# Second feed-forward: one 512-column product for the high and low parts of the token sums

## The chip, the core and the metric

The kernel runs on one core of one Trainium2 chip. The time is device microseconds for one launch of the whole block; the figure for a kernel is the median of several runs. The engines are TensorE (PE, matrix products), VectorE (DVE), ScalarE (ACT), GpSimd (POOL) and SyncE (SP, whose queue issues most of the DMA transfers here).

## What is computed

One layer of a streaming encoder block for 512 frames of width 1024: a feed-forward, a token mixer (a gated delta rule beside latent attention), and a second feed-forward, each behind a normalisation with a learned shift and scale, each added to the input with a gate:

```
x = x + 0.5 * g1 * swiglu(modulate(x, sh1, s1), ffn1_w_in, ffn1_w_out)
x = x + g2 * mixer(modulate(x, sh2, s2))
x = x + 0.5 * g3 * swiglu(modulate(x, sh3, s3), ffn2_w_in, ffn2_w_out)

swiglu(h, w_in, w_out): gate, up = split(h @ w_in); return (silu(gate) * up) @ w_out
```

`w_in` is 1024 x 5632 (2816 gate columns, 2816 up columns), `w_out` 2816 x 1024, all in float32. The change lies in the last line alone.

## The kernel before

Tokens lie along the columns of a tile (512 of them), features along the 128 partitions. Every float32 operand is split in two parts in the type fp32r: a high part by a cast, a low part by subtracting the cast from the original. A product of a 128 x 128 weight tile with an operand is three matmuls: high weight by high operand, high weight by low operand, low weight by high operand. They add up in PSUM, in tiles of 128 x 512 float32. There are eight such tiles: three in the pool that the method `acc` draws from (`pa` in the profile) and five in the pool of `aux` (`pb`).

**The pairs.** The 22 column blocks of gate and up are done one by one. The first four (`PLAIN`) are plain products. For each of the other 18, called pairs here and numbered 0 to 17 (f = 4 to 21 in the code), gate and up of both halves of the tokens are made from seven products of half the depth (four K tiles of 128) and half the width (256 tokens) in place of eight. For this the weight blocks `g` and `u` are loaded by SP into raw tiles (`wr`, 128 x 1024, a ring of four buffers), sums of their halves are made on DVE (`sx`, `sy`: `sums` and `sums2`), and `u`, the sums `x` and `y`, and half of `g` (`g1`) are split into high and low parts (`wh`/`wl`, `yh`/`yl`, `gh`/`gl`): in `pair_tasks`, `hi` is a cast on ACT and `lo` a subtraction on DVE. On the token side four sums `t1` to `t4` of four K tiles each are made once, in `token_sums`, with their high part in a tile `fh` and their low part in a tile `fl`; two sums share a pair of tiles, 256 columns each.

The seven products of a pair are named up0, up1, s2, s3, s1, s4 and gate1. Of these s2, s3, s1 and gate1 use token sums; up0, up1 and s4 use the plain token tiles (`hh`, `hl`). up0, s2, s1 and s4 add up in one half of a PSUM tile `A`; up1 takes one half of a second tile `BC`, and s3 and gate1 the other. On the way the state of `A` is copied out three times (`early_copy`), and `both`, `gate0`, `gate1`, `act1`, `act0` and `act_low` make from these the activation and its two parts (`ah`, `al`).

**The order.** `ffn2_rest` counts in ticks, and a pair begins every seven. `STEPS` says at which tick of a pair each product stands, so that one product of 12 matmuls of 256 columns stands in every tick; between them stand steps of the product with `w_out` (`k_step`: three matmuls of 512 columns into a `pa`). Pairs overlap: a pair's tasks stand from 11 ticks before its start (`load`) to 16 behind it (`act_low`). The list at the end of `pair_tasks` gives the tick of each. Tasks of one tick stand in the order in which they were added, and every engine works through its own instructions in the order of the program. SP's queue too is in order: a load that waits for its raw tile to come free holds all loads behind it. At the end of the pairs, the product with the last six blocks of `w_out` is woven in by the table `last` (`steps_of`), with accumulators from `acc`.

**A transfer that adds.** In earlier stages some low parts are made in another way, and the change uses it too (`split_w`): ACT writes the negated high part to the low tile with an activation (L195), and a DMA issued by POOL adds the raw tile to it (L196).

Lines that matter below, of the kernel before: L267 to L269 are the three matmuls of the product with `w_out`; L787 to L793 the sums of weights; L804 `hi`, L809 `lo`, L816 `early_copy`, L822 `both`, L825 `gate0`, L832 `act1`, L835 and L837 `act0`, L841 `act_low`, L872 to L874 the three matmuls of a product, L899 the addition of a finished column block to the result, L913 and L929 the split of `w_out`, L118 every load on SP.

## Time and profile before

| what | value |
|---|---|
| runs | 1047.45 us median of 3 (1047.32 to 1048.46) |
| profiled execution: its time | 1047.25 us |
| profiled execution: its span | 1045.6 us |
| mean granted TensorE clock | 0.999 |
| PE busy | 1029.0 us, 98% of the span |
| DVE, ACT, POOL busy | 682.6, 448.6, 48.2 us |

The span runs from the first to the last instruction that the profile holds, and the execution's own time has 1.65 us more around it. In a group of instructions, "x" is the count, then come busy time and mean duration, then the idle time of the engine just before. In a timeline the columns are start, duration, engine, line, operation, output and inputs. A duration is from start to end of one instruction; neighbours on one engine overlap a little, so the step from start to start is shorter than the duration. In the windows, "x" counts instructions, and DMA is the mean busy share of the 16 DMA engines. The pairs lie between 734 and 1010 us.

### The profile page before, as it was taken

The numbers are of one execution on the slowest core, as the hardware profiler recorded it, in microseconds if no ns is written. First come the engines' busy times: TensorE is split into PE (matmuls) and PEld (weight loads), VectorE is DVE, ScalarE is ACT, GpSimd is POOL, SyncE is SP. The second block draws the span as 40 slices with busy tenths as digits, with TensorE's granted clock in tenths as the row PEclk, the third lists the DMA queues.
The fourth block names the chain that finished last, engine by engine and source line by source line (L and its number), as shares of the span: only waits on it lengthen the run. The fifth ranks groups of instructions, "written<-read, shape, count | busy, mean of one in ns | idle before, by whom it ended". The sixth has DMA issues, their size and how long they took to land.

```text
span 1045.6 us, 16109 instructions
## 1 busy us (share of the span) xinstructions
PE 1029.0 (98%) x6379; PEld 882.2 (84%) x6379; DVE 682.6 (65%) x1251; ACT 448.6 (43%) x781; POOL 48.2 (5%) x113
## 2 busy tenths in 40 slices
PE   6999999999999999999999999999999999999998
PEld 4778878788887799888778779998999999999986
DVE  4488984333486636648878556788778778777633
ACT  4343222232222226749565464465345444344422
POOL 1000000000000011100010111310000000000000
PEclk9999999999999999999999999999999999999999
DMA  9989973323586439712212201173423334333222
GB/s 274 292 232 322 298 218 101 100 84 94 190 285 220 155 102 231 185 40 54 69 41 56 72 22 41 41 162 101 141 81 102 104 99 121 91 92 109 74 61 81
DMA packets 203689, 136.88 MB, mean 131 GB/s; under 512 B 13777, under 2 KB 186590, under 8 KB 203614
## 3 DMA queue, kind: packets, MB, share of 16 engines
q1 hardware_dynamic: 202318, 131.14, 42.6%
q0 software_dynamic: 1296, 4.72, 2.4%
q8 instruction: 50, 0.82, 0.3%
q14 instruction: 25, 0.20, 0.1%
HBM read 128.63 MB, written 2.49 MB: 125 GB/s over the span
## 4 chain that ended last, share of the span: by engine, by line
PE 90%; ACT 4%; DVE 4%; issue 1%; DMA 1%; POOL 0%; SPq 0%; POOLq 0%; ACTq 0%; DVEq 0%
PE pa L267 20%; PE pa L268 20%; PE pa L269 20%; PE pb L872 6%; PE pb L873 6%; PE pb L874 6%; PE pb L267 1%; PE pb L268 1%; PE pb L269 1%; PE pb L1909 1%; PE pb L418 1%; PE pb L1939 1%; PE pb L1494 1%; DVE cv L1438 1%; PE pb L1912 1%
## 5 line engine op out<-in xcount | busy, mean ns | idle before, releaser
L267 PE MATMUL pa<-hh,wh 128*128 128x512 f32 (+1 forms) x565 | 216.8, 384 | 0.4 <-ACT hh L465 0.4
L193 ACT CAST wh<-wr 128x1024 fp32r<-128x1024 f32 (+1 forms) x106 | 107.9, 1018 | 250.6 <-PE pa L268 177.8
L268 PE MATMUL pa<-hl,wh 128*128 128x512 f32 (+1 forms) x565 | 214.7, 380 | 0.5 <-DVE hl L457 0.3
L269 PE MATMUL pa<-hh,wl 128*128 128x512 f32 (+1 forms) x565 | 214.5, 380 | 0.0
L198 DVE TENSOR_TENSOR wl<-wr,wh 128x1024 fp32r<-128x1024 f32 (+1 forms) x97 | 114.2, 1178 | 104.0 <-ACT wh L193 101.6
L267 PE MATMUL pa<-ah,wh 128*128 128x512 f32 (+1 forms) x396 | 145.5, 368 | 0.6 <-DVE xT L899 0.4
L268 PE MATMUL pa<-al,wh 128*128 128x512 f32 (+1 forms) x396 | 144.5, 365 | 0.0
L269 PE MATMUL pa<-ah,wl 128*128 128x512 f32 (+1 forms) x396 | 143.5, 362 | 0.0
L267 PEld LDWEIGHTS pa<-hh,wh 128*128 128x128 f32 x565 | 106.4, 188 | 23.9 <-issue 3.3
L269 PEld LDWEIGHTS pa<-hh,wl 128*128 128x128 f32 x565 | 106.3, 188 | 20.6 <-issue 0.9
L268 PEld LDWEIGHTS pa<-hl,wh 128*128 128x128 f32 x565 | 106.5, 188 | 19.6 <-DVE hl L457 1.1
L269 PEld LDWEIGHTS pa<-ah,wl 128*128 128x128 f32 x396 | 74.8, 189 | 12.0
L267 PEld LDWEIGHTS pa<-ah,wh 128*128 128x128 f32 x396 | 75.2, 190 | 10.3 <-ACT wh L193 1.7
L268 PEld LDWEIGHTS pa<-al,wh 128*128 128x128 f32 x396 | 75.2, 190 | 7.2
L577 DVE SCALAR_TENSOR_TENSOR aa<-ar,sc,aa 128x512 f32<-128x512 f32 x98 | 72.9, 747 | 8.2 <-DMA ar<-in_w_ada 6.8
L872 PE MATMUL pb<-fh,wh 128*128 128x256 f32 x144 | 40.7, 283 | 0.0
L874 PE MATMUL pb<-fh,wl 128*128 128x256 f32 x144 | 40.7, 283 | 0.0
L874 PE MATMUL pb<-hh,wl 128*128 128x256 f32 x144 | 40.7, 283 | 0.0
L873 PE MATMUL pb<-fl,wh 128*128 128x256 f32 x144 | 40.7, 282 | 0.0
L873 PE MATMUL pb<-hl,wh 128*128 128x256 f32 x144 | 40.7, 282 | 0.0
L899 DVE SCALAR_TENSOR_TENSOR xT<-pa,mod,xT 128x512 f32<-128x512 f32 (+1 forms) x40 | 29.3, 735 | 17.3 <-PE pa L269 17.3
L872 PE MATMUL pb<-hh,wh 128*128 128x256 f32 x144 | 40.6, 282 | 0.0
(445 smaller groups left out, 2003.1 us busy)
## 6 DMA issues: line engine op xcount, KB each, us to landing
wr<-in_ffn_w_in SPq DMA_DIRECT2D x82, 512.0 KB, 3.9
ar<-in_w_ada SPq DMA_DIRECT2D x48, 512.0 KB, 6.1
wr<-in_ffn_w_out SPq DMA_DIRECT2D x34, 512.0 KB, 3.9
ar<-in_w_ada SPq DMA_DIRECT2D x48, 256.0 KB, 4.8
wr<-in_w_in SPq DMA_DIRECT2D x21, 512.0 KB, 4.3
wr<-in_ffn_w_out SPq DMA_DIRECT2D x17, 384.0 KB, 3.4
wl<-wr POOLq DMA_DIRECT2D x9, 512.0 KB, 6.1
wr<-in_w_out SPq DMA_DIRECT2D x8, 512.0 KB, 3.8
```

The lines of the kernel that those rows point to most:

```text
L193: self.nc.scalar.copy(hi, raw)
L198: self.nc.vector.tensor_tensor(out=lo, in0=raw, in1=hi.bitcast(F32), op=ALU.subtract)
L267: mm(out, wh, xh, start=start, stop=False)
L268: mm(out, wh, xl, start=False, stop=False)
L269: mm(out, wl, xh, start=False, stop=stop)
L418: nc.tensor.matmul(pg[32 * q:32 * q + 32, :256], self.sc[:, kc:kc + 1].to_broadcast([P, 32]), a[:, kc], start=(e == 0), stop=(e == 1), til ...
L577: nc.vector.scalar_tensor_tensor(out=acc, in0=a, scalar=sc, in1=acc, op0=ALU.mult, op1=ALU.add)
L872: mm(out, wh, xh, start=start and k == 0, stop=False, **kw)
L873: mm(out, wh, xl, start=False, stop=False, **kw)
L874: mm(out, wl, xh, start=False, stop=stop and k == 3, **kw)
L899: nc.vector.scalar_tensor_tensor(out=self.xT[t][:, ts], in0=p[:, ts], scalar=gate[:, t:t + 1], in1=self.xT[t][:, ts], op0=ALU.mult, op1=AL ...
L1438: nc.vector.scalar_tensor_tensor(out=a[:, d:], in0=p[:, :NT - d], scalar=wj(3 - d), in1=a[:, d:], op0=ALU.mult, op1=ALU.add)
```

## The change

- `token_sums` puts the high part of a token sum into the left half and the low part into the right half of one tile `fb`, one tile for each sum. The cast and the subtraction, one of 512 columns each before, are now two of 256 each.
- `product`: in s2, s3, s1 and gate1 the two matmuls with the high weight part become one of 512 columns, over the whole of `fb`. Its left half collects as before, and its right half collects what the low parts give. The matmul with the low weight part stays, with 256 columns. up0, up1 and s4 stay as they were.
- A PSUM tile now holds a product and its second half: `A` for up0, s2, s1 and s4; `U` (one half used) for up1, from `acc` in pairs with odd f and from `aux` in the others; `G` for s3 and gate1.
- The reads add the halves (`fold`, on DVE). Before, `both` was one operation of 512 columns; now it is three of 256. `gate0` becomes two instead of one, `act1` two instead of one, and the copy `uc` has a fold behind it. The third early copy (`cc`, right half) has a second copy on ACT and an addition on POOL behind it.
- The low part of `u` is no longer a subtraction on DVE: ACT negates `u` and writes it where the low part goes, and a DMA on POOL's queue adds the raw tile (`lo` does nothing for `u`). Here `hi` writes the activation with the scale -1 from the raw tile, in the type of the low part.
- The low part of `g1`, and `act_low` for all pairs but the last two, move from DVE to POOL.

```diff
--- before.py
+++ after.py
@@ -757,18 +757,19 @@
             stt(out=t[:, lo], in0=b[:, hi], scalar=self.dsh[:, k:k + 1], in1=a[:, hi], op0=ALU.add, op1=ALU.subtract)
             stt(out=t[:, hi], in0=b[:, lo], scalar=shift, in1=old[:, hi], op0=ALU.add, op1=ALU.subtract, reverse1=True)
             names = ("t3", "t4")
-        fh, fl = self.slot(F32R, "fh"), self.slot(F32R, "fl")
-        for name, part in zip(names, (lo, hi)):
-            self.T[name].append((fh[:, part], fl[:, part]))
-        nc.scalar.copy(fh, t)
-        yield
-        v.tensor_tensor(out=fl, in0=t, in1=fh.bitcast(F32), op=ALU.subtract)
+        both = [self.slot(F32R, "fb") for _ in range(2)]
+        for name, x, part in zip(names, both, (lo, hi)):
+            self.T[name].append((x[:, lo], x[:, hi], x))
+            nc.scalar.copy(x[:, lo], t[:, part])
+        yield
+        for x, part in zip(both, (lo, hi)):
+            v.tensor_tensor(out=x[:, hi], in0=t[:, part], in1=x[:, lo].bitcast(F32), op=ALU.subtract)
 
     def pair_tasks(self, f, base, add):
 
 
         nc, v, w = self.nc, self.nc.vector, self.ins["ffn2_w_in"][0]
-        r = {}
+        r = {"odd": f % 2}
         flat = lambda t: t.rearrange("p k f -> p (k f)")
         A, B = slice(0, NT), slice(NT, 2 * NT)
 
@@ -802,34 +803,52 @@
                     for e in "hl":
                         r[name + e] = flat(self.wp.tile([P, 8, P], F32R, tag="w" + e, name=self.name("w" + e)))
                 nc.scalar.copy(r[name + "h"], r[src][:, part])
+                if name in 'u':
+                    nc.scalar.activation(r[name + "l"], r[src][:, part], AF.Copy, scale=-1.0)
+                    nc.gpsimd.dma_start(r[name + "l"].bitcast(F32), r[src][:, part], accum_op=ALU.add)
             return go
 
         def lo(name, src, part=slice(0, 2 * NT)):
             def go():
-                v.tensor_tensor(out=r[name + "l"], in0=r[src][:, part], in1=r[name + "h"].bitcast(F32), op=ALU.subtract)
+                if name not in 'u':
+                    eng = nc.gpsimd if name == "g1" else v
+                    eng.tensor_tensor(out=r[name + "l"], in0=r[src][:, part], in1=r[name + "h"].bitcast(F32), op=ALU.subtract)
             return go
 
         def early_copy(name, part):
             def go():
                 if name not in r:
                     r[name] = self.slot(s=name)
-                nc.scalar.copy(r[name][:, part], r["A"][:, :HALF])
+                out = r[name][:, part]
+                nc.scalar.copy(out, r["A"][:, L])
+                if name == "uc":
+                    fold(out, out, r["A"][:, H])
+                elif part is H:
+                    nc.scalar.copy(r["uc"][:, H], r["A"][:, H])
+                    nc.gpsimd.tensor_tensor(out=out, in0=out, in1=r["uc"][:, H], op=ALU.add)
             return go
 
+        def fold(out, a, b):
+            v.tensor_tensor(out=out, in0=a, in1=b, op=ALU.add)
+
         L, H = slice(0, HALF), slice(HALF, NT)
 
         def both():
-            v.tensor_tensor(out=r["cc"], in0=r["cc"], in1=r["BC"], op=ALU.add)
+            for x in (L, H):
+                fold(r["cc"][:, H], r["cc"][:, H], r["G"][:, x])
+            fold(r["cc"][:, L], r["cc"][:, L], r["U"][:, L])
 
         def gate0():
-            v.tensor_tensor(out=r["uc"][:, H], in0=r["uc"][:, L], in1=r["BC"][:, H], op=ALU.add)
+            fold(r["uc"][:, H], r["uc"][:, L], r["G"][:, L])
+            fold(r["uc"][:, H], r["uc"][:, H], r["G"][:, H])
             nc.scalar.activation(r["uc"][:, H], r["uc"][:, H], AF.Silu, scale=-1.0)
 
         def gate1():
             nc.scalar.activation(r["cc"][:, H], r["cc"][:, H], AF.Silu, scale=-1.0)
 
         def act1():
-            v.tensor_tensor(out=r["cc"][:, H], in0=r["cc"][:, H], in1=r["A"][:, :HALF], op=ALU.mult)
+            fold(r["uc"][:, H], r["uc"][:, H], r["A"][:, L])
+            v.tensor_tensor(out=r["cc"][:, H], in0=r["cc"][:, H], in1=r["uc"][:, H], op=ALU.mult)
 
         def act0():
             v.tensor_tensor(out=r["cc"][:, L], in0=r["cc"][:, L], in1=r["uc"][:, H], op=ALU.mult)
@@ -838,7 +857,8 @@
 
         def act_low():
             al = self.slot(F32R, "al")
-            v.tensor_tensor(out=al, in0=r["cc"], in1=r["ah"].bitcast(F32), op=ALU.subtract)
+            eng = nc.gpsimd if f < FT - 2 else v
+            eng.tensor_tensor(out=al, in0=r["cc"], in1=r["ah"].bitcast(F32), op=ALU.subtract)
             self.act.append((r["ah"], al))
 
         r["do"] = dict(load=load, sums=sums, sums2=sums2)
@@ -857,20 +877,28 @@
 
 
         if "A" not in r:
-            r["A"], r["BC"] = self.aux(), self.aux()
+            r["A"] = self.aux()
+        if what == "up1":
+            r["U"] = self.acc() if r["odd"] else self.aux()
+        if what == "s3":
+            r["G"] = self.aux()
         L, H = slice(0, HALF), slice(HALF, NT)
-        b = lambda k0, ts: [(self.h[k][0][:, ts], self.h[k][1][:, ts]) for k in range(k0, k0 + 4)]
+        b = lambda k0, ts: [(self.h[k][0][:, ts], self.h[k][1][:, ts], None) for k in range(k0, k0 + 4)]
         out, w, part, xs, start, stop = {
-            "up0": (r["A"][:, L], "u", 0, b(0, L), True, False), "up1": (r["BC"][:, L], "u", 1, b(4, L), True, True),
-            "s2": (r["A"][:, L], "x", 1, self.T["t2"], False, False), "s3": (r["BC"][:, H], "x", 0, self.T["t3"], True, False),
-            "s1": (r["A"][:, L], "y", 0, self.T["t1"], False, False), "s4": (r["A"][:, L], "y", 1, b(4, H), False, True),
-            "gate1": (r["BC"][:, H], "g1", 0, self.T["t4"], False, True)}[what]
+            "up0": ("A", "u", 0, b(0, L), True, False), "up1": ("U", "u", 1, b(4, L), True, True),
+            "s2": ("A", "x", 1, self.T["t2"], False, False), "s3": ("G", "x", 0, self.T["t3"], True, False),
+            "s1": ("A", "y", 0, self.T["t1"], False, False), "s4": ("A", "y", 1, b(4, H), False, True),
+            "gate1": ("G", "g1", 0, self.T["t4"], False, True)}[what]
         mm, kw = self.nc.tensor.matmul, dict(skip_group_check=True)
-        for k, (xh, xl) in enumerate(xs):
+        wide, out = r[out], r[out][:, L]
+        for k, (xh, xl, both) in enumerate(xs):
             c = slice(part * NT + k * P, part * NT + k * P + P)
             wh, wl = r[w + "h"][:, c], r[w + "l"][:, c]
-            mm(out, wh, xh, start=start and k == 0, stop=False, **kw)
-            mm(out, wh, xl, start=False, stop=False, **kw)
+            if both is None:
+                mm(out, wh, xh, start=start and k == 0, stop=False, **kw)
+                mm(out, wh, xl, start=False, stop=False, **kw)
+            else:
+                mm(wide, wh, both, start=start and k == 0, stop=False, **kw)
             mm(out, wl, xh, start=False, stop=stop and k == 3, **kw)
 
     def ffn2_rest(self, ps):
```

**The products.** First two K tiles of s2 on PE, before (`fh`, `fl` the token sum's parts, `wh`, `wl` the weight's, `pb1416` the tile A):

```order
L872 MATMUL pb1416_7137<-fh1342_6867,wh1395_7070 128x256 [waits Activation_49]
L873 MATMUL pb1416_7137<-fl1343_6868,wh1395_7070 128x256
L874 MATMUL pb1416_7137<-fh1342_6867,wl1396_7071 128x256
L872 MATMUL pb1416_7137<-fh1345_6873,wh1395_7070 128x256
L873 MATMUL pb1416_7137<-fl1346_6874,wh1395_7070 128x256
L874 MATMUL pb1416_7137<-fh1345_6873,wl1396_7071 128x256
```

Now the same two K tiles and the two behind them (`fb` is a sum's tile with both parts):

```order
L901 MATMUL pb1416_7154<-fb1343_6868,wh1395_7085 128x512 [waits Activation_49]
L902 MATMUL pb1416_7154<-fb1343_6868,wl1396_7086 128x256
L901 MATMUL pb1416_7154<-fb1346_6875,wh1395_7085 128x512
L902 MATMUL pb1416_7154<-fb1346_6875,wl1396_7086 128x256
L901 MATMUL pb1416_7154<-fb1349_6884,wh1395_7085 128x512
L902 MATMUL pb1416_7154<-fb1349_6884,wl1396_7086 128x256
```

Three matmuls of 256 columns have become one of 512 and one of 256, with as many columns in all.

**The raw tile of u, pairs 5 and 6.** On DVE before: `wr1490` is the raw u of pair 5, read last by the subtraction L809.

```order
L791 SCALAR_TENSOR_TENSOR sx1496_7728<-sy1497_7729,wr1490_7656 128x512
L793 TENSOR_TENSOR sy1497_7729<-wr1490_7656,sx1496_7728 128x512 [waits DVE_49]
L809 TENSOR_TENSOR wl1503_7753<-wr1490_7656,wh1502_7752 128x1024 [waits Activation_49]
L832 TENSOR_TENSOR cc1482_7608<-cc1482_7608,pb1479_7584 128x256 [waits PE_49,Activation_49]
L809 TENSOR_TENSOR wl1509_7790<-sx1496_7728,wh1508_7789 128x1024 [waits Activation_49]
```

Now on POOL, where the same tile is `wr1493` and its last reader is the DMA that adds it to `wl1506`:

```order
L828 TENSOR_TENSOR cc1484_7605<-cc1484_7605,uc1494_7673 128x256 [waits Activation_49,Pool_49]
L815 TENSOR_TENSOR gl1499_7703<-wr1471_7502,gh1498_7702 128x512 [waits DMAHW2_49,PE_49,Pool_49]
L808 DMA wl1506_7743<-wr1493_7655 128x1024 [waits DMASW3_49,DMAHW5_49,PE_49,Activation_49]
L861 TENSOR_TENSOR al1508_7760<-cc1463_7452,ah1503_7735 128x512 [waits DVE_49]
L828 TENSOR_TENSOR cc1504_7740<-cc1504_7740,uc1516_7798 128x256 [waits Activation_49]
```

SP's loads at that place before; `wr1511` is the raw u of pair 6, and takes the buffer of `wr1490`:

```order
L118 DMA wr1490_7656<-in_ffn2_w_in 128x8x128 [waits DMAHW7_49,DVE_49]
L118 DMA wr1505_7772<-in_ffn2_w_out 128x4x256 [waits DMAHW3_49,DVE_49]
L118 DMA wr1510_7792<-in_ffn2_w_in 128x8x128 [waits DMAHW2_49,DVE_49]
L118 DMA wr1511_7794<-in_ffn2_w_in 128x8x128 [waits DMAHW5_49,DVE_49]
L118 DMA wr1526_7905<-in_ffn2_w_out 128x4x256 [waits DMAHW4_49,DVE_49]
```

And now; `wr1515` is the raw u of pair 6:

```order
L118 DMA wr1493_7655<-in_ffn2_w_in 128x8x128 [waits DMAHW7_49,Activation_49,Pool_49]
L118 DMA wr1509_7765<-in_ffn2_w_out 128x4x256 [waits DMASW5_49,DMAHW3_49,DVE_49,Activation_49]
L118 DMA wr1514_7784<-in_ffn2_w_in 128x8x128 [waits DMAHW2_49,Activation_49,Pool_49]
L118 DMA wr1515_7786<-in_ffn2_w_in 128x8x128 [waits DMASW6_49,DMAHW5_49,DVE_49,Activation_49]
L118 DMA wr1531_7891<-in_ffn2_w_out 128x4x256 [waits DMAHW6_49,DVE_49]
```

The subtraction has left DVE. The load of pair 6's u, which waited for a DVE instruction, now waits for a transfer on POOL's queue to land (`DMASW6`).

**Behind s1 of the last pair.** On PE before, from the last matmul of s1 to the first of `steps_of(2, 0, 2)`:

```order
L874 MATMUL pb1793_9792<-fh1358_6924,yl1786_9728 128x256
L267 MATMUL pa1805_9902<-ah1775_9655,wh1799_9830 128x512
L268 MATMUL pa1805_9902<-al1779_9678,wh1799_9830 128x512
L269 MATMUL pa1805_9902<-ah1775_9655,wl1800_9831 128x512
L267 MATMUL pa1805_9902<-ah1795_9807,wh1799_9830 128x512
L268 MATMUL pa1805_9902<-al1798_9827,wh1799_9830 128x512
L269 MATMUL pa1805_9902<-ah1795_9807,wl1800_9831 128x512
L267 MATMUL pa1809_9938<-ah1731_9329,wh1803_9868 128x512 [waits Activation_49]
```

And now; `pa1814` is U of the last pair (f = 21, odd), and `pa1827` the accumulator that takes its buffer:

```order
L902 MATMUL pb1810_9690<-fb1358_6930,yl1802_9634 128x256
L267 MATMUL pa1823_9793<-ah1790_9559,wh1816_9730 128x512
L268 MATMUL pa1823_9793<-al1795_9587,wh1816_9730 128x512
L269 MATMUL pa1823_9793<-ah1790_9559,wl1817_9731 128x512
L267 MATMUL pa1823_9793<-ah1811_9704,wh1816_9730 128x512
L268 MATMUL pa1823_9793<-al1815_9727,wh1816_9730 128x512
L269 MATMUL pa1823_9793<-ah1811_9704,wl1817_9731 128x512
L267 MATMUL pa1827_9830<-ah1744_9247,wh1820_9766 128x512 [waits DVE_49,Activation_49]
```

On DVE the folds of `both` for that pair stand so now, and the last of them is what the matmul waits for:

```order
L854 TENSOR_TENSOR cc1791_9564<-cc1791_9564,uc1800_9629 128x256
L832 TENSOR_TENSOR cc1812_9709<-cc1812_9709,pb1822_9769 128x256 [waits Pool_49]
L832 TENSOR_TENSOR cc1812_9709<-cc1812_9709,pb1822_9769 128x256 [waits DVE_49]
L832 TENSOR_TENSOR cc1812_9709<-cc1812_9709,pa1814_9714 128x256
L861 TENSOR_TENSOR al1828_9837<-cc1791_9564,ah1826_9825 128x512 [waits Activation_49]
```

The matmul that waited for ACT alone now waits for DVE too; DVE's first fold waits for the addition on POOL.

## The prediction

> **What bounds the kernel now.** I read the busy table first, then the chain of waits by engine, then windows over the pairs, with the slices of the DMA engines kept for later.
>
> ```profile
> PE 1029.0 (98%) x6379; PEld 882.2 (84%) x6379; DVE 682.6 (65%) x1251; ACT 448.6 (43%) x781; POOL 48.2 (5%) x113
> ...
> DMA  9989973323586439712212201173423334333222
> ...
> PE 90%; ACT 4%; DVE 4%; issue 1%; DMA 1%; POOL 0%; SPq 0%; POOLq 0%; ACTq 0%; DVEq 0%
> ```
>
> TensorE is busy for 98% of the span and carries 90% of the chain that ended last. The windows (PE, PEld, DVE, ACT and POOL busy, granted clock, DMA share, GB/s) say the same of the pairs:
>
> ```profile
> 800.00:820.00 20.00, 19.96 (x150) 18.98 (x149) 17.39 (x24) 9.78 (x17) 0.00 (x0) 1.00 0.43 132
> ...
> 840.00:900.00 60.00, 60.00 (x418) 55.99 (x417) 44.91 (x64) 26.09 (x44) 0.00 (x0) 1.00 0.35 105
> ```
>
> PE has no gap between 840 and 900 us, and 0.04 us between 800 and 820. So a gain can come only from less PE time, and what is taken off DVE gains nothing by itself. The other engines matter where they come so late that PE waits. The question is whether the change saves PE more than it makes it wait.
>
> **What PE saves.** The timeline of PE at the end of a step of the product with w_out, through s2, into the next step, and at six of these 512-column matmuls in the tail:
>
> ```profile
> 901.37 0.39 PE L269 MATMUL pa<-ah,wl 128*128 128x512 f32 x1
> 901.60 0.28 PE L872 MATMUL pb<-fh,wh 128*128 128x256 f32 x1
> ...
> 903.03 0.40 PE L267 MATMUL pa<-ah,wh 128*128 128x512 f32 x1
> ...
> 1004.87 0.28 PE L874 MATMUL pb<-fh,yl 128*128 128x256 f32 x1
> 1004.99 0.40 PE L267 MATMUL pa<-ah,wh 128*128 128x512 f32 x1
> ...
> 1006.37 0.39 PE L267 MATMUL pa<-ah,wh 128*128 128x512 f32 x1
> ```
>
> The 0.28 and 0.40 us are lengths; the pace is the step from start to start. Twelve matmuls of 256 columns take 903.03 - 901.60 = 1.43 us, 119 ns each. Six of 512 take 1006.37 - 1004.99 = 1.38 us, 230 ns each, and one with a 256 behind it 0.23 us (901.37 to 901.60). Two of 256 are 238 ns, so the merge saves 8 ns. There are 4 products x 4 K tiles x 18 pairs = 288 such places: 288 x 8 ns = 2.4 us. The starts are given to 10 ns; with a step of 235 ns the saving is 0.9 us, with 226 ns 3.5 us. I take 2.4.
>
> [...]
>
> **What the reads cost.** Durations before, by group (count, busy, mean ns, idle before), of DVE, then ACT, then POOL (in its earlier stages, since POOL does nothing in the pairs):
>
> ```profile
> L822 DVE TENSOR_TENSOR cc<-cc,pb 128x512 f32<-128x512 f32 x15 | 10.2, 679 | 0.0
> L809 DVE TENSOR_TENSOR gl<-wr,gh 128x512 fp32r<-128x512 f32 x15 | 10.4, 691 | 6.0 <-ACT gh L804 6.0
> L841 DVE TENSOR_TENSOR al<-cc,ah 128x512 fp32r<-128x512 f32 x15 | 10.4, 691 | 1.1
> L825 DVE TENSOR_TENSOR uc<-uc,pb 128x256 f32<-128x256 f32 x14 | 5.9, 420 | 23.5 <-PE pb L874 23.5
> ...
> L816 ACT COPY cc<-pb 128x256 f32<-128x256 f32 x30 | 11.0, 366 | 1.7 <-PE pb L874 1.5
> L195 ACT ACTIVATE wl<-wr 128x1024 fp32r<-128x1024 f32 x9 | 9.4, 1044 | 0.0
> ...
> L481 POOL TENSOR_TENSOR na<-na,sq 128x256 f32<-128x256 f32 x9 | 7.8, 868 | 112.0 <-ACT sq L479 111.9
> ```
>
> The starts of the sums of weights below give the pair's period, and show what slack s2 has in an ordinary pair:
>
> ```profile
> 832.90 0.68 DVE L788 TENSOR_TENSOR sx<-wr,wr 128x512 f32<-128x512 f32 x1
> 848.48 0.68 DVE L788 TENSOR_TENSOR sx<-wr,wr 128x512 f32<-128x512 f32 x1
> ...
> 835.61 0.37 ACT L816 COPY cc<-pb 128x256 f32<-128x256 f32 x1
> 836.58 1.06 ACT L804 CAST wh<-wr 128x1024 fp32r<-128x1024 f32 x1 [0.60 <-ACT cc L816]
> ...
> 839.28 0.28 PE L872 MATMUL pb<-fh,wh 128*128 128x256 f32 x1
> ```
>
> The period is 848.48 - 832.90 = 15.58 us. DVE works 44.91 / 60 x 15.58 = 11.7 us of it. The low parts of g1 and of the activation leave it (0.69 each), the low part of u too (1.22, the row of L809 below), and `both` goes from 0.68 to 3 x 0.42. The other folds add 3 x 0.42. Net: 10.9 us. ACT, at 26.09 / 60 x 15.58 = 6.8 us, gains a negation (1.04) and a copy (0.37). POOL gains 2 x 128x512, an addition (0.87) and a DMA issue. All fit in the period, and I cost them at nothing where PE's work covers them: s2 may start when the copy `cc` is done (835.61 + 0.37 = 835.98) but starts at 839.28, so it has 3.3 us of cover. Once that is used up, a delay costs PE its whole length. The two halves in `token_sums` lie ahead of the pairs, under plain products, and I leave them at nothing too.
>
> **The detour of u's low part.** The subtraction becomes a negation and a DMA. Times of the nine such DMAs in earlier stages (issue, and from issue to landing), then those of the loads between 795 and 860 us:
>
> ```profile
> L196 POOL DMA_DIRECT2D wl<-wr x9: 836/848/1038, 395.8 to 690.8; - x9
> ...
> DMA to landing us min/median/max: 4.5/6.1/8.7
> ```
>
> ```profile
> DMA to landing us min/median/max: 3.7/3.8/3.9
> ```
>
> For the product up0 of its own pair this comes early enough. In an ordinary pair the cast of u ends at 837.64 (836.58 + 1.06); with the negation and 6.1 us it lands at 844.8, ahead of up0 at about 848.5. But the raw tile stays held until the landing, and the next pair's u loads into it. That load then lands at 844.8 + 3.8 = 848.6, just when `sx` wants it (848.48). With 8.7 us `sx` would be 2.7 us late, which the 3.3 us of cover still take.
>
> One pair has no cover, since the table of ticks makes pair 4 to 5 short. Rows of SP, DVE, ACT and PE there:
>
> ```profile
> 794.31 5.75 SPq L118 DMA_DIRECT2D wr<-in_ffn_w_in  x2
> ...
> 798.44 1.22 DVE L809 TENSOR_TENSOR wl<-wr,wh 128x1024 fp32r<-128x1024 f32 x1
> 804.88 0.68 DVE L788 TENSOR_TENSOR sx<-wr,wr 128x512 f32<-128x512 f32 x1
> ...
> 796.64 1.05 ACT L804 CAST wh<-wr 128x1024 fp32r<-128x1024 f32 x1
> 807.59 0.36 ACT L816 COPY cc<-pb 128x256 f32<-128x256 f32 x1
> ...
> 808.01 0.39 PE L872 MATMUL pb<-fh,wh 128*128 128x256 f32 x1
> ```
>
> Before, L809 ended at 799.66 and let pair 6's u load go (the second of SP's two, ending at 800.06). Now the cast ends at 797.69, the negation at about 798.7, and the raw tile is free when the DMA has landed: at 803.2 with 4.5 us, at 807.4 with 8.7 us. I take 5.0. The nine were measured in slices where the DMA engines were mostly 7 to 9 tenths busy (slices 16, 17 and 27 of the row DMA above; one slice is 26.1 us), and here the share is 0.43, so I stay near the fast end. Then the load is in at 803.7 + 3.8 = 807.5, and `sx`, at 804.88 before, is 2.6 us late. Queued behind it on DVE are the low part of w_out and `act0`; ACT's `ah` waits for `act0`, the copy `cc` stands behind `ah` on ACT, and s2 waits for the copy: 807.59 + 0.36 = 807.95, and s2 began at 808.01. So the cover is 0.06 us, and PE waits **2.5 us** (2.0 to 6.2).
>
> **The tile U at the end.** In the tail `steps_of(2, 0, 2)` takes the buffer of the last pair's U, and waits until the third fold of `both` has read it. Rows of ACT and DVE, to stand beside PE's rows at 1004.87 to 1006.37:
>
> ```profile
> 1005.19 0.37 ACT L816 COPY cc<-pb 128x256 f32<-128x256 f32 x1 [1.22 <-PE pb L874]
> ...
> 1005.59 0.69 DVE L822 TENSOR_TENSOR cc<-cc,pb 128x512 f32<-128x512 f32 x1 [0.30 <-ACT cc L816]
> ```
>
> s1 ends, the copy stands at 1005.19, the second copy behind it from about 1005.46 to 1005.83, the addition on POOL to 1006.7 (0.87), and three folds of 0.42 with steps of about 0.33 to 1007.8. PE wanted the buffer at 1006.37: it waits about **1.5 us**. With a POOL addition half as long it is 1.1; with one twice as long, 2.4.
>
> **The sum.** -2.4 + 2.5 + 1.5 = +1.6 us, made against the profiled execution of 1047.25: 1048.85. The median of the runs is 0.2 above that execution, so I say 1049.0.
>
> **Rivals.**
>
> *Only the saving* (chance 0.20). The two waits do not come, since loads or buffers fall otherwise than I follow them. For the first that needs a landing before 801.1 us (807.95 would then hold), 2.4 us after the issue, and the shortest of nine was 4.5. For the second it needs another buffer for U. Price: 1047.45 - 2.4 = 1045.0, down to 1043.9 with the upper end of the saving.
>
> *One wait alone, or both with a larger saving* (0.15). The tail's wait alone gives 1047.45 - 2.4 + 1.5 = 1046.5; both with 3.5 us saved, 1048.0.
>
> *The transfer takes as long as the slowest of the nine* (0.12), so that pair 5 waits 6.2 us: 1047.45 - 2.4 + 6.2 + 1.5 = 1052.8. For it speaks that the negated tile is read and written by the transfer while loads run; against it, the share of 0.43. Here too belongs that 512 columns cost PE two times 256 and nothing is saved: 1051.4.
>
> *DVE and POOL block each other* (0.08). POOL now works in the pairs for the first time. The trace has a place where the two overlap, and one where they don't:
>
> ```profile
> 640.12 1.23 DVE L198 TENSOR_TENSOR wl<-wr,wh 128x1024 fp32r<-128x1024 f32 x1
> ...
> 640.28 1.96 POOL L1232 TENSOR_TENSOR Sg<-S,gl 128x512 f32<-128x512 f32 x1
> 646.96 1.04 POOL L1232 TENSOR_TENSOR Sg<-S,gl 128x512 f32<-128x512 f32 x1 [4.72 <-DVE S L1731]
> ```
>
> A 128x512 on POOL took 1.96 in place of 1.04 us beside a DVE subtraction with two inputs in SBUF. If every operation of POOL were stretched so (1.96 + 1.96 + 1.6) and DVE stood still for as long, DVE would need 10.9 + 5.5 = 16.4 us of a period of 15.58; it decides from 4.7 us a pair on. Then 0.8 us x 12 ordinary pairs = 9.8 us come on top: 1058.8. Against it: in that place it was POOL that stretched, and DVE's 1.23 was its usual 1.22. [...]
>
> **Chances.** Forecast 0.45, rivals 0.20, 0.15, 0.12 and 0.08. What a measurement can tell from no change is about 0.2%, or 2.1 us: 1045.35 to 1049.55. Below lies most of the first rival: 0.17. Within lie the second rival, the rest of the first and some 0.28 of the forecast (its own range, by the bounds of its terms without the longest landing, is 1047.5 to 1050.5): 0.46. Above lie 0.17 of the forecast and the last two rivals: 0.37. The range for eight in ten reaches from the first rival, 1044.8, to the third, 1053.0.
>
> **What would show it.** In the profile after: steps of 230 ns for L901 (PE busy lower by some 2 us over the pairs); one wait of PE at s2 of pair 5, near 808 us, with `sx` as the late link and SP's load behind the landing on POOL's queue; one wait of PE near 1006 us for a fold on DVE; no other wait of PE between 734 and 1000 us; DVE near 11 us a pair. Waits in every pair would make the last rival right. No wait at 808 us would mean that the raw tile is not the link that I take it for, and a landing above 6 us that the load on the DMA engines does not explain the spread.

## The result, and the profile after

The changed kernel takes 1051.51 us (median of 18 runs, 1050.03 to 1058.25), the kernel before 1047.53 in the runs beside it: a ratio of 1.0043, with a 95% interval of 1.0035 to 1.0052. It is slower by some 4 us, where 1.6 were forecast. The profiled execution of the changed kernel has a span of 1049.2 us against 1045.6, so there are 3.6 us to find between the two traces. The other 0.4 us of the 4.0 lie outside the spans: the changed kernel's execution has 1051.27 - 1049.2 = 2.07 us around its span, for 1.65 before, and the traces do not show what they are. One execution further below, of the kernel with a raw tile of its own, ran at a granted clock of 0.852 from end to end; it is the one that was profiled, and the ratio leaves it out.

The busy table and the chain of waits by engine, after:

```profile
PE 1028.8 (98%) x6091; PEld 868.6 (83%) x6091; DVE 706.6 (67%) x1297; ACT 468.6 (45%) x825; POOL 126.7 (12%) x183
...
PE 92%; DVE 2%; issue 2%; ACT 2%; DMA 1%; POOL 1%; SPq 0%; POOLq 0%; ACTq 0%; DVEq 0%
```

PE has the 288 matmuls less (6379 - 6091), and its busy time has not moved, though the chain still lies on it. So part of what it saved has come back as slower matmuls, and the span grew by waits on top. The waits of PE behind 734 us (what waited, for whom, total, times, longest):

```profile
PE pb L901 <- ACT cc L823: 3.2, 1, 3.2
PE pa L267 <- ACT cc L847: 1.5, 1, 1.5
PE pa L267 <- DVE xT L927: 0.5, 1, 0.5
PE pb L730 <- DVE xT L927: 0.4, 1, 0.4
```

The last two stood in the kernel before with 0.4 us each. New are one wait of 3.2 us and one of 1.5 us. The first is s2 of pair 5; rows of DVE, ACT, PE and POOL around it:

```profile
802.88 0.68 DVE L788 TENSOR_TENSOR sy<-wr 128x512 f32<-128x512 f32 x1
806.56 1.45 DVE L789 TENSOR_TENSOR sx<-wr,wr 128x512 f32<-128x512 f32 x1 [3.00 <-DMA wr<-in_ffn_w_in]
...
810.03 0.37 ACT L823 COPY cc<-pb 128x256 f32<-128x256 f32 x1
...
810.45 0.50 PE L901 MATMUL pb<-fb,wh 128*128 128x512 f32 x1 [3.24 <-ACT cc L823]
...
797.09 0.86 POOL L808 DMA_DIRECT2D wl<-wr  x1 [1.03 <-ACT wl L807]
806.17 1.29 POOL L815 TENSOR_TENSOR gl<-wr,gh 128x512 fp32r<-128x512 f32 x1
```

The sum `sx` of pair 6 waits for its raw tile's load (3.00 us of idle DVE), and the queue behind it brings s2 late by 3.24 us. Before, s2 began 808.01 - 804.88 = 3.13 us behind `sx`; now it is 810.45 - 806.56 = 3.89 us. The 0.76 us more are `sx` itself, which took 1.45 us for 0.68, beside the low part of g1 on POOL (806.17 to 807.46). So the late load makes some 2.5 us of the pause, and the stretched sum some 0.8.

The second is the matmul behind s1 of the last pair that takes the buffer of U; rows of POOL, DVE and PE:

```profile
1007.81 0.73 POOL L828 TENSOR_TENSOR cc<-cc,uc 128x256 f32<-128x256 f32 x1 [10.56 <-ACT uc L827]
1009.36 0.41 DVE L832 TENSOR_TENSOR cc<-cc,pa 128x256 f32<-128x256 f32 x1
1009.92 0.47 PE L267 MATMUL pa<-ah,wh 128*128 128x512 f32 x1 [1.49 <-ACT cc L847]
```

The third fold, which reads U, ends at 1009.77. The view names an ACT instruction (L847) because that one ended last; a run below shows that the matmul does not need it.

Behind the first pause comes what was not foreseen. Windows of one microsecond over the restart; the number behind POOL's busy time is the granted clock:

```profile
810.00:811.00 1.00, 0.55 (x3) 0.51 (x4) 1.00 (x3) 1.00 (x3) 0.00 (x0) 0.97 0.55 110
811.00:812.00 1.00, 1.00 (x5) 0.81 (x4) 0.97 (x3) 1.00 (x2) 0.00 (x0) 0.50 1.08 382
812.00:813.00 1.00, 1.00 (x5) 0.90 (x4) 0.61 (x2) 1.00 (x3) 0.40 (x1) 0.50 1.14 341
813.00:814.00 1.00, 1.00 (x3) 0.77 (x3) 0.22 (x2) 1.00 (x3) 1.00 (x2) 0.50 0.91 216
814.00:815.00 1.00, 1.00 (x5) 0.81 (x4) 1.00 (x2) 0.76 (x1) 0.79 (x1) 0.82 1.02 197
```

The clock is at half from about 810.94 (0.97 as a mean over a microsecond) to 814.36 (0.82): 3.42 us. What it costs is read from the steps of PE inside and behind it:

```profile
812.14 0.63 PE L901 MATMUL pb<-fb,wh 128*128 128x512 f32 x1
812.78 0.63 PE L267 MATMUL pa<-ah,wh 128*128 128x512 f32 x1
...
815.23 0.40 PE L901 MATMUL pb<-fb,wh 128*128 128x512 f32 x1
815.58 0.40 PE L901 MATMUL pb<-fb,wh 128*128 128x512 f32 x1
```

A wide matmul with the narrow one behind it takes 0.64 us at half clock and 0.35 at full, so 3.42 us do the work of 1.87, a loss of about 1.6 us. The other pairs run as planned. For the pace I compare the first matmul of up0 in pair 1 and in pair 17, before and after:

```profile
746.66 0.28 PE L872 MATMUL pb<-hh,wh 128*128 128x256 f32 x1
990.78 0.28 PE L872 MATMUL pb<-hh,wh 128*128 128x256 f32 x1
```

```profile
746.49 0.28 PE L898 MATMUL pb<-hh,wh 128*128 128x256 f32 x1
836.57 0.28 PE L898 MATMUL pb<-hh,wh 128*128 128x256 f32 x1
851.97 0.28 PE L898 MATMUL pb<-hh,wh 128*128 128x256 f32 x1
992.80 0.28 PE L898 MATMUL pb<-hh,wh 128*128 128x256 f32 x1
```

The stretch from pair 1 to pair 17 took 244.12 us and takes 246.31. An ordinary pair's period fell from 15.58 to 15.40 or 15.41 us (851.97 - 836.57 = 15.40), so 0.17 to 0.18 us a pair, 10.5 ns for each of 16 merged places, 3.0 us for 288. The bill: -3.0 + 3.2 + 1.6 + 1.5 = +3.3 of the 3.6 us of the spans. The remaining 0.3 us are not placed; at the start of pair 1 the two executions already differ by 0.2 us.

### The profile page after: what moved, and what is told of

Its sections match the earlier page's. It is cut to its first block, busy times and chain, and to the rows that moved or that the text cites. A ratio compares the mean times of both kernels' runs of the same rounds, so it can differ in the third digit from the quotient of the medians.

```text
span 1049.2 us, 15808 instructions
## 1 busy us (share of the span) xinstructions
PE 1028.8 (98%) x6091; PEld 868.6 (83%) x6091; DVE 706.6 (67%) x1297; ACT 468.6 (45%) x825; POOL 126.7 (12%) x183
## 4 chain that ended last, share of the span: by engine, by line
PE 92%; DVE 2%; issue 2%; ACT 2%; DMA 1%; POOL 1%; SPq 0%; POOLq 0%; ACTq 0%; DVEq 0%
PE pa L267 21%; PE pa L268 21%; PE pa L269 21%; PE pb L901 6%; PE pb L902 5%; PE pb L899 2%; PE pb L898 2%; PE pb L267 1%; PE pb L269 1%; PE pb L268 1%; PE pb L1937 1%; PE pb L418 1%; PE pb L1967 1%; PE pb L1522 1%; PE pb L1940 1%
## 5 line engine op out<-in xcount | busy, mean ns | idle before, releaser
L901 PE MATMUL pb<-fb,wh 128*128 128x512 f32 x144 | 52.8, 401 | 3.2 <-ACT cc L823 3.2
L832 DVE TENSOR_TENSOR uc<-uc,pb 128x256 f32<-128x256 f32 x72 | 29.9, 415 | 28.8 <-ACT uc L823 16.6
L902 PE MATMUL pb<-fb,wl 128*128 128x256 f32 x144 | 40.6, 282 | 0.0
L844 ACT ACTIVATE uc<-uc 128x256 f32<-128x256 f32 x18 | 7.5, 418 | 69.1 <-DVE uc L832 69.1
L623 DVE TENSOR_TENSOR af<-sg,pa 128x512 f32<-128x512 f32 x19 | 13.0, 685 | 35.6 <-PE pa L269 35.5
L901 PEld LDWEIGHTS pb<-fb,wh 128*128 128x128 f32 x144 | 27.3, 190 | 9.8 <-ACT cc L823 3.4
```

What stands on the lines that cost most here:

```text
L832: v.tensor_tensor(out=out, in0=a, in1=b, op=ALU.add)
L901: mm(wide, wh, both, start=start and k == 0, stop=False, **kw)
L902: mm(out, wl, xh, start=False, stop=stop and k == 3, **kw)
```

## The experiments

The theory after these traces: the product is worth 3.0 us; the transfer that makes u's low part holds a raw tile too long in the one short pair, which costs PE a long pause and, behind it, half the clock for 3.4 us; and the tile U costs 1.5 us in the tail. The rivals: that the folds and POOL make DVE late by themselves, that the low clock has another cause, and that the tail's wait would be there in any case. Each run has its own runs of the kernel before beside it, and ratios are to these. "The stretch" is from pair 1's up0 to pair 17's, as above: 244.12 before, 246.31 after.

**u's low part on DVE in pair 5 alone.**

```diff
-                if name in 'u':
+                if name == 'u' and f != 9:
                     nc.scalar.activation(r[name + "l"], r[src][:, part], AF.Copy, scale=-1.0)
...
-                if name not in 'u':
+                if name != 'u' or f == 9:
```

> The changed kernel, but in pair 5 alone the low part of u is again a subtraction on DVE (17 pairs keep the transfer). Theory (the raw tile of u, held until the transfer lands, makes pair 6's load late, and nothing else makes the one long pause): PE's wait of 3.2 us at s2 of pair 5 goes, and with it the stretch of about 3.4 us behind it at a granted clock of 0.5, which costs some 1.5 us; 1051.5 falls to about 1046.8 us, and the tail's wait of 1.5 us stays. Rival (DVE itself is late in pair 5, since it has three folds and POOL beside it): the wait stays above 2 us and the time within 1 us of 1051.5.

1048.38 us, ratio 1.0006 (0.9997 to 1.0015); stretch 243.05. PE's waits in the pairs and the tail:

```profile
PE pa L267 <- ACT cc L847: 1.5, 1, 1.5
PE pb L901 <- ACT cc L823: 0.8, 1, 0.8
PE pb L898 <- ACT uc L827: 0.5, 1, 0.5
```

One transfer of 18 taken back removes 3.3 us of the stretch. The clock stays at 1.0 (its window from 800 to 820 us has a mean of 1.00, against 0.91). So the detour in this one pair is the main cause; that it acts by the held tile, the last run of this section shows. But the time is 1.6 us over the 1046.8 expected, and 0.8 + 0.5 us of waits remain, which the theory did not have: with three folds more and POOL beside it, DVE is late in this short pair without any transfer too. In this run's timeline `sy` (L794) took 1.67 us for 0.69, beside L861 on POOL, and `act0` (L854) 0.96 for 0.41, beside L828. The rival is right to that extent.

**U of the last pair from the other pool.**

```diff
-        r = {"odd": f % 2}
+        r = {"odd": f % 2, "last": f == FT - 1}
...
-            r["U"] = self.acc() if r["odd"] else self.aux()
+            r["U"] = self.acc() if r["odd"] and not r["last"] else self.aux()
```

> The changed kernel, but U of the last pair comes from the pool of five tiles and no longer from that of three. Theory (the wait near 1007 us is for this buffer): that wait of 1.5 us goes and the time falls by 1.5 us to about 1050.0. Rival (PE waits there for the chain of copies and folds in any case, by the matmuls behind): the wait moves to the next instruction and the time stays at 1051.5.

1050.36 us, ratio 1.0023 (1.0014 to 1.0033). The wait in the tail is gone, not moved; the long pause stays:

```profile
PE pb L901 <- ACT cc L823: 3.2, 1, 3.2
PE pa L267 <- DVE xT L927: 0.5, 1, 0.5
```

From pair 17 to the end of the span it is 54.7 us, against 56.4 in the changed kernel and 54.8 before. The matmul now begins at 1008.54, ahead of the ACT instruction L847 (1009.76 here), so in the changed kernel it waited for the buffer and not for ACT. The rival falls.

**The low parts of g1 and of the activation on DVE again.**

```diff
-                    eng = nc.gpsimd if name == "g1" else v
+                    eng = v
...
-            eng = nc.gpsimd if f < FT - 2 else v
+            eng = v
```

> The changed kernel, but the low parts of g1 and of the activation are on DVE as before the change, so that POOL has the short addition and the transfers alone. Theory A (POOL and DVE hold each other up: the sum sx of pair 6 took 1.45 us in place of 0.68 beside the low part of g1 on POOL): that sum takes 0.68 again, the pause at s2 of pair 5 shrinks from 3.2 to about 2.5 us, and a shorter pause may leave the clock at 1.0; 1050.8 if the clock still falls, 1049.2 if it doesn't. Theory B (the DVE time saved is needed): DVE at 12.3 us a pair becomes late elsewhere, and the time is 1051.5 or more.

1052.7 us (median of four), ratio 1.0047 (1.0032 to 1.0062); stretch 247.13. The sum `sx` of pair 6 took 0.69 us again, as theory A had it, but the pause shrank only to 2.85 us, and the clock fell all the same. For that case theory A gave 1050.8, which is 1.9 us too low: a new wait of 0.6 us came in for the transfer itself, in up0 of pair 5, and pair 16 took 0.45 us longer (15.86 us for 15.41). The time lies in the range of theory B, yet is not told apart from the changed kernel's, so the run decides nothing between the two on time. But its trace shows what the two moves did to DVE. Groups of DVE between 780 and 1000 us, first of the changed kernel, then of this one, then windows of the two (DVE's busy time is the third of the five):

```profile
L851 DVE TENSOR_TENSOR cc<-cc,uc 128x256 f32<-128x256 f32 x15 | 22.7, 1516 | 2.1 <-ACT cc L847 0.8
L789 DVE TENSOR_TENSOR sx<-wr,wr 128x512 f32<-128x512 f32 x14 | 16.2, 1156 | 15.9 <-DMA wr<-in_ffn_w_in 15.9
...
900.00:960.00 60.00, 60.00 (x357) 53.08 (x356) 55.10 (x73) 29.91 (x50) 17.36 (x16) 1.00 0.56 144
```

```profile
L789 DVE TENSOR_TENSOR sx<-wr,wr 128x512 f32<-128x512 f32 x14 | 11.8, 840 | 1.8 <-DMA wr<-in_ffn_w_in 1.8
L851 DVE TENSOR_TENSOR cc<-cc,uc 128x256 f32<-128x256 f32 x15 | 6.4, 426 | 1.5
...
900.00:960.00 60.00, 60.00 (x358) 53.13 (x357) 49.36 (x78) 30.42 (x48) 6.85 (x8) 1.00 0.54 141
```

With the two operations on POOL, DVE works 55.10 / 60 x 15.41 = 14.2 us a pair; with both back on DVE, 12.7. Over 840 to 960 us it is 13.8 and 12.6. Moving 1.4 us of work off DVE made DVE busier by 1.2 to 1.5 us, because other operations of DVE stretch beside POOL's: L851 from 0.43 to 1.52, `sx` from 0.84 to 1.16.

**More matmuls in the pause.** Ahead of s2 of pair 5, into a half of U that nobody reads, on data that lie ready:

```diff
+                    if j == 5 and STEPS[s - 7 * j] == "s2":
+                        for i in range(24):
+                            nc.tensor.matmul(pairs[j]["U"][:, HALF:], pairs[j]["uh"][:, i % 4 * P:i % 4 * P + P],
+                                             self.h[i % 4][0][:, HALF:], start=True, stop=True, skip_group_check=True)
                     self.product(pairs[j], STEPS[s - 7 * j])
```

> The changed kernel with 24 more matmuls of 256 columns ahead of s2 of pair 5, into an unused half of a PSUM tile, on data that lie ready; they take 24 x 0.119 = 2.9 us and fall into the pause of 3.2 us. Theory (the pause lowers the granted clock, and the matmuls behind it pay): the clock stays at 1.0 behind it, and the time falls by about 1.5 us to 1050.0 although PE does more. Rival (the low clock has another cause, such as the transfers that run there): the clock falls as before, and the time is 1051.5 or a little more.

1050.16 us, ratio 1.0023 (1.0012 to 1.0034); stretch 244.68, which is 1.6 us shorter than the changed kernel's, with 24 matmuls more. The window over the place, with PE's remaining wait of 0.4 us in it:

```profile
800.00:820.00 20.00, 19.63 (x127) 17.73 (x126) 16.00 (x23) 9.09 (x17) 5.45 (x5) 1.00 0.61 150
```

The clock held, with the transfers running as before. All eight executions have a mean clock of 0.999 or 1.000 over the span, where 17 of the changed kernel's 18 have 0.998 or less. It is the pause that lowers it.

The same with 8 and with 16 of these matmuls, one execution each:

> As with the 24 further matmuls, but 8 of them (0.95 us), so that about 2.3 us of the pause are left. Theory (a pause has to be long to lower the clock; after 1.5 us in the tail it did not fall, after 2.8 us it did): if the bound lies above 2.3 us the clock stays at 1.0, and the stretch from pair 1 to pair 17 is 244.6 us as with 24; if below, the clock falls to 0.5 for 3.4 us and the stretch stays at 246.3.

> As with the 24 further matmuls, but 16 of them (1.9 us), so that about 1.3 us of the pause are left, shorter than the tail's wait of 1.5 us, behind which the clock held. Theory: the clock stays at 1.0, and the stretch from pair 1 to pair 17 is 244.6 us. Rival (the clock goes by the share of busy time over a longer stretch, not by one pause): it falls here too, and the stretch is near 246.

With 8 a pause of 2.28 us is left and the clock holds; with 16 one of 1.3 us, and it holds too (1050.63 and 1050.14 us, stretches 244.95 and 244.68). Windows with 8:

```profile
811.00:812.00 1.00, 0.83 (x5) 0.74 (x6) 0.96 (x3) 1.00 (x3) 0.00 (x0) 1.00 0.82 227
812.00:814.00 2.00, 2.00 (x12) 1.68 (x11) 1.40 (x3) 2.00 (x4) 0.68 (x2) 1.00 1.12 346
```

So in these executions the bound lies between 2.3 and 2.85 us. It need not be a fixed one: the clock fell 3.7 us behind the pause's beginning in one trace and 2.35 in another (see the last section), and each length was seen in one trace alone.

**The transfer alone, on the kernel before.**

```diff
                 nc.scalar.copy(r[name + "h"], r[src][:, part])
+                if name == 'u':
+                    nc.scalar.activation(r[name + "l"], r[src][:, part], AF.Copy, scale=-1.0)
+                    nc.gpsimd.dma_start(r[name + "l"].bitcast(F32), r[src][:, part], accum_op=ALU.add)
...
             def go():
+                if name == 'u':
+                    return
                 v.tensor_tensor(out=r[name + "l"], in0=r[src][:, part], in1=r[name + "h"].bitcast(F32), op=ALU.subtract)
```

> The kernel before with one part of the change alone: u's low part by negation on ACT and the adding transfer; products, reads and POOL as before. Theory (the raw tile held until the landing makes the pause by itself): one wait of PE at s2 of pair 5, about 2.5 us since no work on POOL stretches the sum sx, with a stretch at half clock behind it, none in the tail, none elsewhere; 1047.5 + 2.5 + 1.6 = about 1051.6 us. Rival (the pause comes from the folds and POOL, and the transfer is hidden): no wait, 1047.5.

1052.55 us, ratio 1.0048 (1.0031 to 1.0065); stretch 248.94, which is 4.8 us over the kernel before. PE's wait, and two of the windows behind it:

```profile
PE pb L877 <- ACT cc L821: 3.3, 1, 3.3
...
814.00:815.00 1.00, 1.00 (x4) 0.80 (x4) 0.42 (x1) 1.00 (x3) 0.86 (x1) 0.50 0.04 10
815.00:816.00 1.00, 1.00 (x3) 0.76 (x3) 0.94 (x1) 1.00 (x3) 0.00 (x0) 0.50 0.68 131
```

Without a fold and without the new product the pause and the half clock are there, 3.3 + 1.6 = 4.9 us for the expected 4.1. The rival, a hidden transfer, falls. No other pair waits. That the pause is as long as the changed kernel's is chance: here `sx` takes its usual 0.69 us, but begins 9.2 us behind the transfer's issue (799.59 to 808.80).

**u's low part on DVE in all pairs, and everything on DVE.** The first leaves out negation and transfer for all pairs; the second also takes the low parts of g1 and of the activation, and the addition to `cc`, from POOL to DVE.

> The changed kernel with u's low part on DVE in all pairs (no negation, no transfer). Theory (the transfer costs only in pair 5): like the kernel with the subtraction in pair 5 alone, short waits of about 1.3 us in all near pair 5 and the tail's 1.5 us, no half clock; 1047.5 - 3.0 + 1.3 + 1.5 = 1047.3. Rival (the detour's relief of DVE is needed in every pair): DVE at 12.1 us a pair is late in ordinary pairs too, and the time is over 1050.

> The wide product with its reads, and nothing moved: u's, g1's and the activation's low parts and the added right half of cc are on DVE, and POOL has no work in the pairs. DVE needs about 13.9 us of a period of 15.4. Theory (PE waits only in the short pair, where DVE's queue decides): no wait in ordinary pairs; some waits near pair 5 and the tail's 1.5 us, in all 3 to 5 us against 3.0 saved: 1047.5 to 1049.5. Rival (DVE's queue is late throughout, and the moves pay): waits in most pairs, over 1055.

The first: 1048.12 us, ratio 1.0004 (0.9994 to 1.0013), stretch 242.99, with the waits of the kernel that has pair 5 alone on DVE. The transfer in the 17 other pairs thus bought nothing that PE could use. The second: 1056.23 us, ratio 1.0081 (1.0066 to 1.0096), stretch 250.69:

```profile
PE pb L901 <- ACT cc L823: 4.6, 3, 3.0
PE pa L267 <- ACT cc L847: 2.2, 1, 2.2
PE pb L898 <- ACT uc L827: 0.9, 1, 0.9
...
800.00:820.00 20.00, 16.09 (x83) 13.73 (x82) 17.17 (x28) 9.36 (x16) 0.00 (x0) 0.83 0.35 104
840.00:900.00 60.00, 60.00 (x361) 53.29 (x361) 51.95 (x86) 27.00 (x47) 0.00 (x0) 1.00 0.35 106
...
L828 DVE TENSOR_TENSOR cc<-cc,uc 128x256 f32<-128x256 f32 x15 | 6.4, 426 | 24.9 <-ACT uc L827 24.8
```

The time is the rival's, over 1055, but its mechanism is not there: between 840 and 960 us PE does not wait (60.00 of 60 us in the window shown), and behind that only some 0.5 us in pair 16. The theory's size fails: the short pairs and the tail cost more than the 3 to 5 us allowed, 7.7 us in the rows of waits, and a mean clock of 0.83 over 20 us is 6.8 us at half, some 3 us more. DVE is not the bound of an ordinary pair; it is late in the short ones, by what its queue holds there. Its busy time is not the reason: it is 51.95 / 60 x 15.41 = 13.3 us a pair, no more than in the changed kernel in the same window (52.64 / 60 x 15.41 = 13.5), which has 3.0 us of work less on DVE. But DVE now stands idle ahead of the addition to `cc` (L828), 24.8 us in 15 pairs, until ACT's copy is there, and what stands behind it waits too. Between this run and the one before lie 8.1 us, so the three operations on POOL do pay, in the short pairs and the tail; which of the three does it was not run.

**Both places mended.** The first two edits together.

> The changed kernel with u's low part of pair 5 on DVE and U of the last pair from the pool of five. Theory: neither the long pause nor the tail's wait, but the short waits near pair 5 of about 1.3 us; 1047.5 - 3.0 + 1.3 = 1045.8, with a little for the clock. Rival (one wait taken away calls another): 1047 or more.

> The kernel with both places mended once more, in more rounds and on the chip of the kernel with the extra raw tile. Theory: 1 us under the kernel before, as the stretch from pair 1 to pair 17 says in its trace (243.2 us against 244.1), so 1046.6 where the kernel before has 1047.6. Rival: no difference from the kernel before.

1046.74 us, ratio 0.9992 (0.9982 to 1.0001), and again 1046.83, ratio 0.9992 (0.9983 to 1.0001); stretches 243.17 and 243.02. The interval just takes in 1 both times; the medians are 1.0 and 0.9 us under the kernel before, in the direction and near the size of the traces (1.0 and 1.1 us in the stretch). PE's waits in the pairs are now 0.8 and 0.5 us, with no half clock behind them.

**A raw tile of its own for u of pair 6, and U from the other pool.** All transfers stay; the load that waited has a further buffer, paid for with two of the 56 general tiles.

```diff
-                t = self.wp.tile([P, 8, P], F32, tag="wr", name=self.name("wr"))
+                if n == "u" and f == 10:
+                    t = self.ws.tile([P, 8, P], F32, tag="wx", name=self.name("wx"), bufs=1)
+                else:
+                    t = self.wp.tile([P, 8, P], F32, tag="wr", name=self.name("wr"))
```

> The changed kernel with all its transfers, with U of the last pair from the pool of five, and with a raw tile of its own for u of pair 6 (the room comes from two of the 56 general tiles). Theory (the cost at pair 5 is that the raw tile is held): pair 6's load no longer waits for the landing, DVE has no subtraction of u either, and PE's waits near pair 5 fall below 0.5 us in all, with the clock at 1.0; 1047.5 - 3.0 + 0.4 = about 1045 us, the best of all. Rival (the folds, and DVE and POOL beside each other, make DVE late there in any case): 1 us of waits stays, and the time is that of the kernel with both places mended, 1046.5 or more.

1046.45 us, ratio 0.9989 (0.998 to 0.9998), the best of all and just clear of the kernel before; it is not told apart from the kernel with both places mended. Against the kernel with U from the other pool alone (1050.36) it is 3.9 us faster, with every transfer and negation in place and only the tile added (and two general tiles fewer), so it is the held tile that costs. Its trace shows the link: the load of pair 6's u is issued at 863.28, ahead of pair 5's transfer at 863.91, and `sx` takes 0.68 us without a wait. The time is short of the 1045 expected, and the rival's 1 us of waits is not excluded. How much of the rest is waiting near pair 5 stays open, since PE's waits in that trace can't be set beside the others.

## Why the prediction was right and where it was not

*What bounds the kernel, and that only PE time counts*: right. DVE's share went up, and the ordinary pairs show no wait.

*What PE saves*: the mechanism was right, the term a little small: 3.0 us for the 2.4 forecast, 10.5 ns a place for 8, and inside the 0.9 to 3.5 given. The starts that I had are rounded to 10 ns, which is as much as the thing measured; the period of a pair over many pairs would have given a better price only afterwards.

*What the reads cost*: nothing in ordinary pairs, as said. But the sum behind it failed. I had DVE at 10.9 us a pair and it was 13.5 between 840 and 900 us and 14.2 between 900 and 960. The step took durations from a trace in which POOL was idle, and kept the stretching of DVE beside POOL for the last rival, at 0.08. That rival's mechanism is there in every pair; its price isn't, since 14.2 us still fit into 15.4. What I wrote against it, that it was POOL that stretched, does not hold in the pairs: there DVE's L851 took 1.52 us in the mean for 0.43, and POOL's L815 took 1.29 to 2.27.

*The detour*: place, chain and count of waits were right: one wait, at s2 of pair 5, with `sx` as the late link. Its size was 3.24 us for 2.5. The transfer was issued at 797.09 and landed after 5.2 us, for the 5.0 taken; the load behind it was issued then, and `sx` began at 806.56, 9.5 us after the issue for the forecast 8.8. That is partly made up for, since the cast of u came earlier (794.79 for 796.64, where up0 came only 0.8 us earlier): the late load makes the forecast 2.5 us. The 0.8 us on top are the stretched `sx`, a term that the sum did not have. The 18 transfers landed in 4.5 to 7.1 us, with a median of 4.7, so staying near the fast end of the nine landings was right; that the DMA share is the reason was not tested.

*What was missing*: the half clock behind the pause, 1.6 us. It is the largest error, and no rival had it: I took a pause of PE at its length alone. In the runs one of 2.28 us left the clock at 1.0, and one of 2.85 was already enough to lower it. Beside these two, my own range for the pause (2.0 to 6.2 us) would have had a second step of about 1.6 us at its upper part.

*The tail*: right in place, cause and size: 1.5 us, for the buffer of U, behind the addition on POOL (1007.81 to 1008.54) and three folds.

The sum in the prediction's own terms is then -3.0 + 3.2 + 1.6 + 1.5 = +3.3, in place of -2.4 + 2.5 + 1.5 = +1.6. The measured 1051.5 lies above the forecast's own range of 1047.5 to 1050.5, which is narrower than the ends of its terms give: with 0.9 us saved and 2.4 in the tail, the same pause of 2.5 us ends at 1051.5. It lies inside the wide range only because the third rival had stretched that to 1053.0, and this is luck: the rival's two prices come near (1052.8 and 1051.4), but the landing was short, and the merge did save.

## What to carry to other kernels

When an operand is given to a slower maker, ask who else waits for the buffers it holds while it is made: the cost here was not in the value's own use but in the next load into its raw tile, in the one pair of 18 without slack. A pause of PE had two prices here, its length and what the clock took back around it; the second came at 2.85 us and more, and was 1.6 us, and once some 3. And moving element-wise work from DVE to POOL may make DVE busier (here by 1.2 to 1.5 us a pair), so measure DVE's operations again beside a working POOL before counting the gain. Such a move can still pay (the three on POOL were worth 8.1 us here), where the operation would stand in DVE's queue and wait there for another engine.

## What the runs showed of the hardware

In the pairs and the tail the granted clock went to 0.50 at pauses of 3.24, 3.3 and 2.85 us. Around one of 3.2 us, with U from the other pool, its mean over 800 to 820 us was 0.91, as in the changed kernel, and around one of 2.97 us, with everything on DVE, 0.83. It stayed at 1.0 behind pauses of 2.28, 1.5 and 1.3 us. At the start of the span PE waits for a load for 3.3 us before and 3.9 us after, and there the clock reads 1.00, from 0 to 20 us. In three of these traces the low stretch lasted 3.42 us, worked out from the means of its first and last windows: 810.94 to 814.36 in the changed kernel, 812.88 to 816.30 with the transfer alone, and in the kernel with the low parts on DVE 810.68 to 814.10, from these two windows:

```profile
810.00:811.00 1.00, 0.00 (x0) 0.00 (x0) 0.97 (x4) 0.76 (x2) 0.00 (x0) 0.84 0.03 9
...
814.00:815.00 1.00, 1.00 (x6) 0.83 (x6) 0.54 (x3) 1.00 (x3) 0.20 (x1) 0.95 0.34 66
```

There the clock fell 0.5 us ahead of PE's restart at 811.18; in the changed kernel it fell 0.5 us behind the restart at 810.45. Behind the pause's beginning these are 2.35 and 3.7 us, so in these two traces it does not fall at a fixed time behind it. In the kernel with everything on DVE the pause of 2.97 us ended at 813.56, 0.8 us behind the fall, and the low stretch, taken at 0.50 like the others, lasted 6.82 us, from 812.74 to 819.56, twice as long as in the three:

```profile
812.00:813.00 1.00, 0.00 (x0) 0.00 (x0) 0.97 (x4) 0.38 (x1) 0.00 (x0) 0.87 0.76 268
...
819.00:820.00 1.00, 1.00 (x6) 0.86 (x5) 1.00 (x2) 0.00 (x0) 0.00 (x0) 0.72 0.97 291
```

What sets these lengths, and the place where the clock falls, the runs do not show.

The runs of the changed kernel spread from 1050.03 to 1058.25 us, with mean clocks from 1.000 to 0.993, and one of the four of the kernel with the low parts on DVE has 1.000 (1050.89 us, its fastest). A stretch of 3.42 us at half alone makes the mean 0.998, so in the two runs with 1.000 the clock seems not to have fallen; but only one run of each kernel has a trace, so this is worked out and not shown.

The other thing is how far POOL and DVE hold each other up. On POOL a 128x512 subtraction took 1.5 to 1.6 us in the mean in the pairs, where DVE works beside it:

```profile
L861 POOL TENSOR_TENSOR al<-cc,ah 128x512 fp32r<-128x512 f32 x15 | 24.2, 1611 | 0.0
L815 POOL TENSOR_TENSOR gl<-wr,gh 128x512 fp32r<-128x512 f32 x15 | 22.9, 1528 | 0.0
```

On DVE in those same pairs a 128x256 operation with two inputs in SBUF took 1.52 us (L851), against 0.43 with the low parts on DVE, while the folds, with one input in PSUM, kept their 0.41, also beside a working POOL (two of them took 0.88 us together from 794.84, in L815's time on POOL from 794.76 to 796.06). That L815 took 1.30 us. The one from 747.43 took 2.27, beside two operations of DVE with both inputs in SBUF, of which DVE's L815 of `yl` (from 747.08) took 1.47 us and L788 (from 748.58) 1.67, for means of 1.21 and 0.72 between 780 and 1000 us. The 1.04 us on POOL in the kernel before (L1232 at 646.96) also had DVE beside them, in L2121 with one input in PSUM (from 646.80 for 0.75 us). So in the changed kernel's trace both engines took longer beside each other.
